# A two-layer decoder trunk on one core: load order, a fourth weight buffer, finer side turns and a later low split

## The chip, the cores and the metric

The kernel runs on one core of a Trainium2 chip. The metric is device time in microseconds for one execution; here the median of three runs. A second figure, the span, is the time from the first to the last instruction of one profiled execution.

## The reference

Input: `x`, 256 tokens of 4096 channels, in float32. Two layers, each with a normalisation ahead of it and a residual sum behind it, then a final normalisation.

```
x = x + even_mixer(rmsnorm(x))     # layer 0
x = x + odd_mixer(rmsnorm(x))      # layer 1
out = rmsnorm(x)

even_mixer(h): u, z_a, qkv, z_b = split(h @ w_in)          # 4096 -> 12288
    y = gelu(s5(u));  y = y * sigmoid(y @ glu_w + b)       # 64 complex state spaces
    o = windowed attention, 8 heads, 3 dilations, merged
    return concat(y * silu(z_a), o * silu(z_b)) @ w_out    # 2048 -> 4096
odd_mixer(h): c_q, c_kv, k_r, k_i, w_i, gate = split(h @ w_in)   # 4096 -> 6336
    indexer: 32 heads score every visible key; each query keeps 64
    32-head attention over the kept latent keys and values
    return (o * silu(gate)) @ w_out                        # 4096 -> 4096
```

`s5(u)` runs a linear complex recurrence over the 256 positions per state: rotate, scan, rotate back, project with C.

## The kernel before

All weight products go through one list of steps. A chunk is up to 1024 output columns of one weight matrix; a step is one chunk's share of 128 rows of the contraction (of 256 or 512 where `kper` is 2 or 4). The chunks in order: `u` (the S5 input), `h0` to `h9` (queries, keys, values and gates of the eight heads, ten 128-column units a head, eight a chunk), `z`, `glu`, `eo0` to `eo3` (even output), `a1`, `a2`, `a3`, `g0`, `iq0` to `iq3` (indexer queries), `g1` to `g3`, then `uq`, `uk`, `uv` for eight groups of four heads, and `oo0` to `oo4` (odd output). Most chunks have 32 steps.

Float32 products are made of three passes. A weight tile `wr` (128 x 1024, 512 KB) is loaded on SyncE's queue (`dma`, L311), rounded to `wh` on ScalarE and the remainder `wl = wr - wh` taken on VectorE (`split`, L322, through `split_to`, L388, at L394 and L399). TensorE then adds `wh` with `xh`, `wl` with `xh`, and `wh` with `xl` into PSUM, for two halves of 128 tokens (`products`, L370): twelve 512-column matmuls a step. `wr`, `wh` and `wl` have three buffers each.

The main loop (L1628) does in step i: split step i+2, load step i+3, let the side jobs advance, and multiply step i. Each engine runs its instructions in this program order.

Everything else is side work, written as generators (`Side`, L222). A job has a rate; `advance` adds the rate to its account and runs the generator to its next `yield` (a turn) for each whole unit. `advance` is left out in the first and the last step of a chunk of eight steps or more, so a 32-step chunk has 30 advances. `finish` runs a job to its end at once. Side matmuls go to two PSUM banks; the chunks rotate over the other six. The side jobs that matter here:

- `x_gen` (L860) brings `x` transposed, in eight pieces of four 128-row tiles, multiplies each piece by the norm weight on POOL, and splits it into `xh`, `xl`. `sums_gen` (L499) loads `x` again as 1 MB tiles `xs` and squares them on ScalarE.
- `s5_main` (L686) handles 32 pairs of groups in batches of four: `s5_tables` and `s5_operands` for the next batch, then per pair two turns on VectorE (rotate; scan and rotate back into `sf`), then the projection with `cpad` and the gelu.
- `even_head` (L764) does rope, scores, softmax, values, transposes into `mhb`/`mlb` for one head, at rate 0.56.
- `idx_all` (L1222) transposes and scores the indexer heads; `mla_all` (L1411) runs the 32 attention heads in five stages, two turns a step.

At a chunk's end its `evac` function empties the PSUM banks; `evac_heads` (L893) first calls `finish` on heads whose place in `ring` is needed. `finish_token` (L1555) is the final norm of 128 tokens.

Of the kernel before, what the change touches and what calls it, by code (L numbers as in the profile page):

```python
# [14 lines left out]
D = 4096  # L15
L = 256
# [108 lines left out]
def lay_out(inp):  # L125
# [71 lines left out]
    a['cpad'] = blockdiag(f['s5_c_re'][0].transpose(0, 2, 1), f['s5_c_im'][0].transpose(0, 2, 1)).reshape(128, 2048)  # L197
# [10 lines left out]
    'mk': (128, 768), 'ident': (128, 128), 'bpad': (8, 128, 256), 'cpad': (128, 2048),  # L208
# [49 lines left out]
def _build(nc, tc, t, debug):  # L258
    from contextlib import ExitStack
    ctx = ExitStack()  # L260
    with ctx:
# [44 lines left out]
        raw, hl = {}, {}  # L306

# [3 lines left out]
        def dma(i, parts=1):  # L311
            c, s, _, _ = steps[i]
            wd = c.kper * c.ncols
            r = st.tile([128, wd], F32, name="wr", tag="wr", bufs=3)
# [7 lines left out]
        def split(i, parts=1):  # L322
# [9 lines left out]
            for k in range(parts):  # L332
                cs = slice(k * wd // parts, (k + 1) * wd // parts)
                split_to(h[:, cs], l[:, cs], r[:, cs])
            hl[i] = (h, l)

# [144 lines left out]
        cpad = big.tile([128, NPAIR, 2, 32], F32, name="cpad", tag="mha")  # L481
# [6 lines left out]
        def x_dma(i, k0=0, k1=4):  # L488
            if k0 == 0:
                xpiece[i] = e.tile([128, 1024], F32, name="xp", tag="SP", bufs=2)  # L490
            DMA.dma_start(xpiece[i][:, k0 * L:k1 * L], t['xT'][i][:, k0 * L:k1 * L])
# [52 lines left out]
        bps = {}  # L544

        def bp_dma(b4):
            bp = e.tile([128, 4, 2, 32], F32, name="bp")
            DMA.dma_start(bp, t['bpad'][b4].rearrange("p (a r c) -> p a r c", a=4, r=2))
            bps[b4] = bp
# [74 lines left out]
        def s5_operands(b4):  # L624
# [6 lines left out]
            for w, (src, second, low) in enumerate(((bk[:, 0:L], 1, 2), (yT[:, b4, :], 2, 1))):  # L631
                A.activation(hi[:, w], src, AF.Copy)
                for j in range(4):
                    A.activation(stk[0:32, w, j, :], src[32 * j:32 * j + 32], AF.Copy)
                for j in range(4):
                    rows = slice(32 * j, 32 * j + 32)
                    V.tensor_tensor(stk[32 * low:32 * low + 32, w, j, :], src[rows], hi[rows, w].bitcast(F32), op=OP.subtract)
                G.tensor_copy(stk[32 * second:32 * second + 32, w], stk[0:32, w])
                yield
# [46 lines left out]
        def s5_main(stage):  # L686
# [10 lines left out]
            V.tensor_scalar(cpad[:, :, 1], cpad[:, :, 1], -1.0, None, op0=OP.mult)  # L697
# [3 lines left out]
            for b4 in range(8):  # L701
# [3 lines left out]
                sfs = []  # L705
                for j in range(4):
# [13 lines left out]
                    V.tensor_tensor(m2[:, 0], bu[:, 1], tab[:, 1], op=OP.mult)  # L720
                    V.tensor_tensor(m2[:, 1], bu[:, 0], tab[:, 1], op=OP.mult)
# [6 lines left out]
                    sf = e.tile([128, 2, L], F32, name="sf", bufs=4)  # L728
                    V.tensor_tensor(sf, sc, cc, op=OP.mult)
                    V.tensor_tensor(m2[:, 0], sc[:, 1], tab[:, 1], op=OP.mult)  # L730
                    V.tensor_tensor(m2[:, 1], sc[:, 0], tab[:, 1], op=OP.mult)
                    V.tensor_tensor(sf[:, 0], sf[:, 0], m2[:, 0], op=OP.subtract)
                    V.tensor_tensor(sf[:, 1], sf[:, 1], m2[:, 1], op=OP.add)
                    sfs.append(sf)
# [6 lines left out]
                for r in range(2):  # L741
                    for j in range(4):
                        rows = slice(32 * j, 32 * j + 32)
                        T.matmul(bk[rows, :L], cpad[:, 4 * b4 + j, r, :], sfs[j][:, r, :], start=(r == 0), stop=(r == 1))
# [5 lines left out]
                A.activation(g1, y, AF.Square)  # L750
                V.tensor_scalar(g1, g1, 0.044715, 1.0, op0=OP.mult, op1=OP.add)
                V.tensor_tensor(g1, g1, y, op=OP.mult)
                A.activation(g2, g1, AF.Tanh, scale=math.sqrt(2.0 / math.pi))

# [9 lines left out]
        def even_head(h, stage):  # L764
# [11 lines left out]
            A.activation(zt, zs, AF.Tanh, scale=0.5)  # L776
            V.scalar_tensor_tensor(zs, zt, 1.0, zs, op0=OP.add, op1=OP.mult)
# [27 lines left out]
            for g in range(3):  # L805
                if g + 1 < 3:
# [9 lines left out]
                         accum_out=sm[:, 1, 1:2])  # L816
            V.reciprocal(sm[:, 2], sm[:, 1])
# [42 lines left out]
        def x_gen():  # L860
            cur['xdone'] = 0
            for i in range(1, 8):
                if i + 1 < 8:
                    x_dma(i + 1)
                p = xpiece[i].rearrange("p (k c) -> p k c", k=4)
                G.tensor_tensor(p, p, spc('ge')[:, 4 * i:4 * i + 4, None].to_broadcast([128, 4, L]), op=OP.mult)
                yield
                for k in (0, 2):
                    kt = slice(4 * i + k, 4 * i + k + 2)
                    split_to(xh[:, kt, :], xl[:, kt, :], p[:, k:k + 2])  # L870
                cur['xdone'] = i
                yield

        def begin_u():
# [3 lines left out]
            cur['x'] = side.add(x_gen(), 1.0)  # L878
# [783 lines left out]
```

## Time and profile before

| | |
|---|---|
| median of 3 runs | 2704.45 us (2704.15 to 2708.99) |
| the profiled execution | 2706.62 us |
| its span | 2704.8 us |
| TensorE busy | 2662.6 us, 98% |
| VectorE, ScalarE, POOL busy | 1709.4, 1224.1, 427.1 us |

The profiled execution's time stands beside its span; the difference is what lies around the span. TensorE's busy time is the union of its matmuls, which are pipelined and overlap, so a busy TensorE may still be slowed within. In the windows view a line gives the stretch, its length, the busy us (and count) of TensorE's matmuls, its weight loads, VectorE, ScalarE and POOL, then granted clock, DMA share and GB/s. Chunk u runs from 5.94 to 107.61 us, h1 to z from 196.85 to 1159.97, iq0 to iq3 from 1652.18 to 1785.14, g2 from 1880.62 to 1967.66, oo4 from 2646.96 to 2692.29. In the waits view, `A <- B: t, n, m` is who waited for whom, the total, the times, the longest.

### The profile page before, as it was taken

What the parts mean: (1) busy time and instruction counts of PE and PEld (TensorE: products, weight loads), DVE (VectorE), ACT (ScalarE), POOL (GpSimd) and SP (SyncE); (2) the same over time, 40 slices, a digit from 0 to 9 for tenths busy, and PEclk for the clock granted to TensorE, in tenths of its full rate; (3) what the DMA queues carried; (4) which work ended last, traced back from release to release, by engine and by line L of the source; (5) the groups of instructions that cost most, each with busy time, mean ns of one, the idle gap of its engine ahead of it and who ended that gap; (6) DMA issues with size and microseconds to landing.
All of it is one profiled execution on the core that took longest, in us unless ns stands there. A gap on an engine that the chain in (4) does not pass through costs nothing.

```text
span 2704.8 us, 33706 instructions
## 1 busy us (share of the span) xinstructions
PE 2662.6 (98%) x12464; PEld 2199.3 (81%) x12464; DVE 1709.4 (63%) x2575; ACT 1224.1 (45%) x1606; POOL 427.1 (16%) x509
## 2 busy tenths in 40 slices
PE   8999999999999999999999999999999999999997
PEld 6787878888887888888888888778888888888886
DVE  5478787877878787465554455556455666654554
ACT  4543444444444444444444444544344555443443
POOL 4214232331323331000000011100000000000000
PEclk9999999999999999999999999999999999999999
DMA  7655545545555455557655556545666444456565
GB/s 267 240 192 182 189 164 179 174 168 170 195 183 171 166 171 178 179 187 264 218 202 189 179 187 223 182 164 191 208 209 206 161 156 163 153 189 226 192 225 197
DMA packets 145061, 516.35 MB, mean 191 GB/s; under 512 B 15872, under 2 KB 17536, under 8 KB 144768
## 3 DMA queue, kind: packets, MB, share of 16 engines
q1 hardware_dynamic: 142368, 504.77, 55.4%
q0 software_dynamic: 2240, 8.39, 0.8%
q8 instruction: 97, 1.59, 0.2%
q10 hardware_dynamic: 288, 1.05, 0.1%
q14 instruction: 68, 0.56, 0.1%
HBM read 501.56 MB, written 12.58 MB: 190 GB/s over the span
## 4 chain that ended last, share of the span: by engine, by line
PE 90%; DVE 4%; DMA 3%; ACT 2%; issue 1%; SPq 0%; POOL 0%; ACTq 0%; DVEq 0%; POOLq 0%
PE bank L382 27%; PE bank L381 27%; PE bank L385 27%; DMA wr<-w_even_in 2%; DVE wl L399 2%; PE bank L367 1%; ACT wh L394 1%; PE bank L1431 1%; DVE sc L727 0%; DMA wr<-w_odd_out 0%; PE bank L834 0%; PE bank L1448 0%; PE bank L787 0%; PE bank L797 0%; DMA wr<-w_iq 0%
## 5 line engine op out<-in xcount | busy, mean ns | idle before, releaser
L399 DVE TENSOR_TENSOR wl<-wr,wh 128x1024 fp32r<-128x1024 f32 (+2 forms) x907 | 1137.4, 1258 | 884.0 <-ACT wh L394 881.1
L394 ACT ACTIVATE wh<-wr 128x1024 fp32r<-128x1024 f32 (+2 forms) x907 | 954.0, 1053 | 1294.6 <-PE bank L385 1041.9
L381 PE MATMUL bank<-wh,xh 128*128 128x512 f32 x1536 | 613.6, 399 | 7.2 <-ACT wh L394 4.1
L382 PE MATMUL bank<-wl,xh 128*128 128x512 f32 x1536 | 602.6, 392 | 13.3 <-DVE wl L399 13.0
L385 PE MATMUL bank<-wh,xl 128*128 128x512 f32 x1536 | 475.0, 390 | 0.0
L382 PEld LDWEIGHTS bank<-wl,xh 128*128 128x128 f32 x1536 | 289.3, 188 | 77.9 <-DVE wl L399 21.5
L381 PEld LDWEIGHTS bank<-wh,xh 128*128 128x128 f32 x1536 | 289.1, 188 | 70.2 <-ACT wh L394 5.9
L385 PEld LDWEIGHTS bank<-wh,xl 128*128 128x128 f32 x1536 | 288.8, 188 | 62.6
L381 PE MATMUL bank<-wh,x2h 128*128 128x512 f32 (+1 forms) x832 | 318.7, 383 | 0.0
L382 PE MATMUL bank<-wl,x2h 128*128 128x512 f32 (+1 forms) x832 | 316.5, 380 | 0.0
L385 PE MATMUL bank<-wh,x2l 128*128 128x512 f32 (+1 forms) x832 | 254.0, 380 | 0.0
L381 PE MATMUL bank<-wh,oh 128*128 128x512 f32 x488 | 191.9, 393 | 0.0
L382 PE MATMUL bank<-wl,oh 128*128 128x512 f32 x488 | 190.4, 390 | 1.1 <-DVE wl L399 1.1
L385 PEld LDWEIGHTS bank<-wh,x2l 128*128 128x128 f32 x832 | 156.5, 188 | 30.2
L381 PEld LDWEIGHTS bank<-wh,x2h 128*128 128x128 f32 x832 | 156.5, 188 | 29.6
L382 PEld LDWEIGHTS bank<-wl,x2h 128*128 128x128 f32 x832 | 156.6, 188 | 29.4
L385 PE MATMUL bank<-wh,ol 128*128 128x512 f32 x488 | 158.9, 389 | 0.0
L382 PEld LDWEIGHTS bank<-wl,oh 128*128 128x128 f32 x488 | 91.7, 188 | 20.9 <-DVE wl L399 2.3
L385 PEld LDWEIGHTS bank<-wh,ol 128*128 128x128 f32 x488 | 91.6, 188 | 19.3
L381 PEld LDWEIGHTS bank<-wh,oh 128*128 128x128 f32 x488 | 91.7, 188 | 18.9 <-ACT v L450 0.4
L381 PE MATMUL bank<-wh,cb_h 128*128 128x512 f32 (+1 forms) x224 | 87.9, 393 | 0.0
L382 PE MATMUL bank<-wl,cb_h 128*128 128x512 f32 (+1 forms) x224 | 84.0, 375 | 0.0
(395 smaller groups left out, 3069.2 us busy)
## 6 DMA issues: line engine op xcount, KB each, us to landing
wr<-w_even_in SPq DMA_DIRECT2D x383, 512.0 KB, 3.4
wr<-w_odd_in SPq DMA_DIRECT2D x192, 512.0 KB, 3.2
wr<-w_odd_out SPq DMA_DIRECT2D x128, 512.0 KB, 3.5
wr<-w_even_out SPq DMA_DIRECT2D x64, 512.0 KB, 3.8
wr<-w_iq SPq DMA_DIRECT2D x48, 512.0 KB, 3.4
wr<-w_uq SPq DMA_DIRECT2D x48, 512.0 KB, 3.4
wr<-w_uv SPq DMA_DIRECT2D x16, 512.0 KB, 3.3
wr<-w_uk SPq DMA_DIRECT2D x16, 384.0 KB, 3.1
```

Of the source, the lines that this page charges most:

```text
L367: T.matmul(c.banks[0][b], hp, hls[k][:, b * 512:b * 512 + 512], start=f0 and k == 0, stop=l0 and k == 1)
L381: T.matmul(acc, xh[:, tok], h[:, b0 + o:b0 + o + n_], start=f0, stop=False)
L382: T.matmul(acc, xh[:, tok], l[:, b0 + o:b0 + o + n_], start=False, stop=False)
L385: T.matmul(acc, xl[:, tok], h[:, b0 + o:b0 + o + n_], start=False, stop=l0)
L394: A.activation(hi, src, AF.Copy)
L399: V.tensor_tensor(lo, src, hi.bitcast(F32), op=OP.subtract)
L1431: T.matmul(bk[:, 128:384], o[:, 0, 128:256], o[:, 1, :], start=True, stop=True)
```

## The change

- Start: the first piece of `x` and the norm weights are loaded on ScalarE's queue; the second weight tile is loaded and split in halves, right behind the first; the rest of `sp` comes later. `wr` has four buffers, and step i loads step i+4.
- `split` issues only `wh`; the subtract for `wl` (`low`) is issued behind the side jobs' turn of the same step.
- `x_gen` leaves out POOL's multiply; the norm weight is applied in the split of each quarter, two quarters a turn, at rate 0.7 and first in the list of jobs.
- S5: turns are cut smaller and the rate is 0.96 in place of 0.5; C comes in eight loads `cb` beside those of B, negated on POOL; `sf` becomes one tile `sfs`; the operand's low part is subtracted once for 128 rows and copied in 32-row pieces on ScalarE.
- `even_head` has two more `yield`s at the same rate. The indexer's rate is 1.0, and a group of four waits until four steps after its `evac`.
- `oo4` loads its residual at k = 8; five of six small steps of the final norm move from POOL to VectorE.

```diff
@@ -304,6 +306,7 @@
         raw, hl = {}, {}
+        now = [0]
@@ -311,7 +314,7 @@
             wd = c.kper * c.ncols
-            r = st.tile([128, wd], F32, name="wr", tag="wr", bufs=3)
+            r = st.tile([128, wd], F32, name="wr", tag="wr", bufs=4)
@@ -331,8 +334,16 @@
                 cs = slice(k * wd // parts, (k + 1) * wd // parts)
-                split_to(h[:, cs], l[:, cs], r[:, cs])
+                A.activation(h[:, cs], r[:, cs], AF.Copy)
             hl[i] = (h, l)
+
+            def low():
+                for k in range(parts):
+                    cs = slice(k * wd // parts, (k + 1) * wd // parts)
+                    V.tensor_tensor(l[:, cs], r[:, cs], h[:, cs].bitcast(F32), op=OP.subtract)
+            if parts > 1:
+                low()
+            return low
@@ -478,7 +489,7 @@
         mk = cp.tile([128, 3, 256], F32, name="mk", tag="mk")
-        cpad = big.tile([128, NPAIR, 2, 32], F32, name="cpad", tag="mha")
+        sfs = big.tile([128, 4, 2, L], F32, name="sfs", tag="mha")
@@ -488,7 +499,7 @@
                 xpiece[i] = e.tile([128, 1024], F32, name="xp", tag="SP", bufs=2)
-            DMA.dma_start(xpiece[i][:, k0 * L:k1 * L], t['xT'][i][:, k0 * L:k1 * L])
+            (A if i == 0 else DMA).dma_start(xpiece[i][:, k0 * L:k1 * L], t['xT'][i][:, k0 * L:k1 * L])
@@ -541,12 +552,14 @@
-        bps = {}
+        bps, cbs = {}, {}
...
             DMA.dma_start(bp, t['bpad'][b4].rearrange("p (a r c) -> p a r c", a=4, r=2))
-            bps[b4] = bp
+            cb = e.tile([128, 4, 2, 32], F32, name="cb", bufs=3)
+            DMA.dma_start(cb, t['cpad'][b4].rearrange("p (a r c) -> p a r c", a=4, r=2))
+            bps[b4], cbs[b4] = bp, cb
@@ -629,14 +642,14 @@
             for w, (src, second, low) in enumerate(((bk[:, 0:L], 1, 2), (yT[:, b4, :], 2, 1))):
-                A.activation(hi[:, w], src, AF.Copy)
-                for j in range(4):
-                    A.activation(stk[0:32, w, j, :], src[32 * j:32 * j + 32], AF.Copy)
-                for j in range(4):
-                    rows = slice(32 * j, 32 * j + 32)
-                    V.tensor_tensor(stk[32 * low:32 * low + 32, w, j, :], src[rows], hi[rows, w].bitcast(F32), op=OP.subtract)
+                lo = e.tile([128, L], F32R, name="ulo")
+                split_to(hi[:, w], lo, src)
+                yield
+                for k, part in ((0, hi[:, w]), (low, lo)):
+                    for j in range(4):
+                        A.activation(stk[32 * k:32 * k + 32, w, j, :], part[32 * j:32 * j + 32].bitcast(F32), AF.Copy)
+                    yield
                 G.tensor_copy(stk[32 * second:32 * second + 32, w], stk[0:32, w])
-                yield
@@ -694,7 +707,6 @@
             yield from s5_tables(0)
-            V.tensor_scalar(cpad[:, :, 1], cpad[:, :, 1], -1.0, None, op0=OP.mult)
@@ -702,7 +714,7 @@
                         yield
-                sfs = []
+                G.tensor_scalar(cbs[b4][:, :, 1], cbs[b4][:, :, 1], -1.0, None, op0=OP.mult)
@@ -718,6 +730,7 @@
                     V.tensor_tensor(m2[:, 0], bu[:, 1], tab[:, 1], op=OP.mult)
+                    yield
@@ -725,13 +738,14 @@
                         V.tensor_tensor_scan(sc[:, r], mg, m1[:, r], 0.0, op0=OP.mult, op1=OP.add)
-                    sf = e.tile([128, 2, L], F32, name="sf", bufs=4)
+                    yield
+                    sf = sfs[:, j]
...
                     V.tensor_tensor(m2[:, 0], sc[:, 1], tab[:, 1], op=OP.mult)
+                    yield
...
                     V.tensor_tensor(sf[:, 1], sf[:, 1], m2[:, 1], op=OP.add)
-                    sfs.append(sf)
@@ -741,16 +755,18 @@
                         rows = slice(32 * j, 32 * j + 32)
-                        T.matmul(bk[rows, :L], cpad[:, 4 * b4 + j, r, :], sfs[j][:, r, :], start=(r == 0), stop=(r == 1))
+                        T.matmul(bk[rows, :L], cbs[b4][:, j, r, :], sfs[:, j, r, :], start=(r == 0), stop=(r == 1))
...
                 A.activation(g1, y, AF.Square)
+                yield
...
                 A.activation(g2, g1, AF.Tanh, scale=math.sqrt(2.0 / math.pi))
+                yield
@@ -774,6 +790,7 @@
             A.activation(zt, zs, AF.Tanh, scale=0.5)
+            yield
@@ -814,6 +831,7 @@
                          accum_out=sm[:, 1, 1:2])
+            yield
@@ -862,29 +880,26 @@
                     x_dma(i + 1)
-                p = xpiece[i].rearrange("p (k c) -> p k c", k=4)
-                G.tensor_tensor(p, p, spc('ge')[:, 4 * i:4 * i + 4, None].to_broadcast([128, 4, L]), op=OP.mult)
-                yield
                 for k in (0, 2):
-                    kt = slice(4 * i + k, 4 * i + k + 2)
-                    split_to(xh[:, kt, :], xl[:, kt, :], p[:, k:k + 2])
-                cur['xdone'] = i
-                yield
+                    split_all([(xh[:, 4 * i + j, :], xl[:, 4 * i + j, :], xpiece[i][:, j * L:(j + 1) * L], spc('ge', 4 * i + j))
+                               for j in (k, k + 1)])
+                    if k == 2:
+                        cur['xdone'] = i
+                    yield
...
             cur['sums'] = side.add(sums_gen(), 0.8)
-            cur['x'] = side.add(x_gen(), 1.0)
+            cur['x'] = side.add(x_gen(), 0.7, first=True)
...
             evac_scaled(c, lambda q: stage[:, q], rstd)
-            DMA.dma_start(cpad, t['cpad'].rearrange("p (a r c) -> p a r c", a=NPAIR, r=2))
             DMA.dma_start(mk, t['mk'].rearrange("p (g c) -> p g c", g=3))
-            s5['job'] = side.add(s5_main(stage), 0.5)
+            s5['job'] = side.add(s5_main(stage), 0.96)
@@ -1256,7 +1271,7 @@
-                        for _ in range(5):
+                        while now[0] < od['iat'] + 4:
@@ -1274,7 +1289,7 @@
                     od['iready'] = od['itr'] = 0
-                    od['ij'] = side.add(idx_all(), 1.4)
+                    od['ij'] = side.add(idx_all(), 1.0)
@@ -1283,7 +1298,7 @@
                 stage = o.tile([128, 1536], F32, name="iqs", tag="Q", bufs=2)
-                lo = o.tile([64, 2, 512], F32, name="iqlo")
+                lo = o.tile([64, 2, 512], F32, name="iqlo", tag="sq")
@@ -1296,7 +1311,7 @@
                 od['iq', i] = stage
-                od['iready'] = i + 1
+                od['iready'], od['iat'] = i + 1, now[0]
@@ -1509,7 +1524,7 @@
                     side.step(u['j'])
-                if k == 20:
+                if k == (8 if i == 4 else 20):
@@ -1560,12 +1575,12 @@
             V.tensor_reduce(v, ss[:, q, :], op=OP.add, axis=mybir.AxisListType.X)
-            G.tensor_scalar(v, v, 1.0 / D, EPS, op0=OP.mult, op1=OP.add)
+            V.tensor_scalar(v, v, 1.0 / D, EPS, op0=OP.mult, op1=OP.add)
             G.tensor_tensor(y, v, mhalf[:, 0:1], op=OP.pow)
-            G.tensor_tensor(a, y, y, op=OP.mult)
-            G.tensor_tensor(a, a, v, op=OP.mult)
-            G.tensor_scalar(a, a, -0.5, 1.5, op0=OP.mult, op1=OP.add)
-            G.tensor_tensor(y, y, a, op=OP.mult)
+            V.tensor_tensor(a, y, y, op=OP.mult)
+            V.tensor_tensor(a, a, v, op=OP.mult)
+            V.tensor_scalar(a, a, -0.5, 1.5, op0=OP.mult, op1=OP.add)
+            V.tensor_tensor(y, y, a, op=OP.mult)
@@ -1604,14 +1619,15 @@
         a0, b0 = SP['ge']
-        DMA.dma_start(sp[:, a0:b0], t['sp'][:, a0:b0])
         x_dma(0, 0, 1)
+        A.dma_start(sp[:, a0:b0], t['sp'][:, a0:b0])
         dma(0, 2)
+        dma(1, 2)
         x_dma(0, 1, 4)
-        DMA.dma_start(sp[:, b0:], t['sp'][:, b0:])
-        dma(1)
...
         x_dma(1)
+        dma(3)
+        DMA.dma_start(sp[:, b0:], t['sp'][:, b0:])
@@ -1623,18 +1639,21 @@
         x_split(0, 1, 4)
-        split(1)
+        split(1, 2)
...
             c, s, first, last = steps[i]
-            if i + 2 < n:
-                split(i + 2)
-            if i + 3 < n:
-                dma(i + 3)
+            now[0] = i
+            low = split(i + 2) if i + 2 < n else None
+            if i + 4 < n:
+                dma(i + 4)
...
                 side.advance()
+
+            if low:
+                low()
```

## Rows read from the trace of the kernel before

**Rows 1.** The page: busy time, share of the span and count of each engine.

```profile
PE 2662.6 (98%) x12464; PEld 2199.3 (81%) x12464; DVE 1709.4 (63%) x2575; ACT 1224.1 (45%) x1606; POOL 427.1 (16%) x509
```

**Rows 2.** Windows by stage: u; h1 to z; iq0 to iq3; g2; oo4.

```profile
5.94:107.61 101.67, 92.83 (x387) 72.83 (x385) 56.35 (x59) 52.37 (x69) 45.55 (x75) 0.98 0.73 262
...
196.85:1159.97 963.12, 951.41 (x4471) 779.46 (x4470) 735.56 (x1243) 420.95 (x527) 266.81 (x275) 1.00 0.53 176
...
1652.18:1785.14 132.96, 129.57 (x584) 103.38 (x582) 80.84 (x96) 71.64 (x98) 18.72 (x14) 1.00 0.60 197
1880.62:1967.66 87.04, 87.04 (x386) 72.10 (x384) 42.96 (x39) 37.30 (x39) 1.13 (x2) 1.00 0.60 206
...
2646.96:2692.29 45.33, 43.84 (x192) 35.77 (x191) 22.53 (x23) 17.95 (x20) 4.08 (x8) 1.00 0.54 178
```

**Rows 3.** Waits of TensorE in u: total us, times, longest.

```profile
PE bank L382 <- DVE wl L399: 4.5, 6, 1.5
PE bank L381 <- ACT wh L394: 4.1, 3, 2.7
```

**Rows 4.** Waits in u of ScalarE and of SyncE's queue.

```profile
ACT wh L394 <- DMA wr<-w_even_in: 37.2, 21, 6.4
...
SPq L319 <- DVE wl L399: 42.6, 24, 6.6
```

**Rows 5.** Waits of TensorE in h1 to z.

```profile
PE bank L382 <- DVE wl L399: 8.5, 7, 1.8
PE bank L381 <- DVE ring L456: 3.1, 4, 1.0
```

**Rows 6.** Timeline of VectorE, an S5 turn: start, us, line, operation, tiles.

```profile
245.74 1.27 DVE L727 TENSOR_TENSOR_SCAN sc<-s5mag,m 128x256 f32<-128x256 f32 x2
...
247.98 0.42 DVE L731 TENSOR_TENSOR m<-sc,tab 128x256 f32<-128x256 f32 x1
...
248.65 1.28 DVE L733 TENSOR_TENSOR sf<-sf,m 128x256 f32<-128x256 f32 x1
249.86 3.19 DVE L399 TENSOR_TENSOR wl<-wr,wh 128x1024 fp32r<-128x1024 f32 x2
```

**Rows 7.** Timeline of TensorE at the start.

```profile
1.44 5.45 PE L1622 MATMUL bank<-warm 128*128 128x512 f32 x6 [1.44 <-DVE warm L1620]
5.94 1.19 PE L381 MATMUL bank<-wh,xh 128*128 128x512 f32 x1
...
10.70 0.49 PE L381 MATMUL bank<-wh,xh 128*128 128x512 f32 x1 [1.05 <-ACT wh L394]
11.95 0.50 PE L382 MATMUL bank<-wl,xh 128*128 128x512 f32 x1 [0.76 <-DVE wl L399]
```

**Rows 8.** Instructions on tile xp: count, ns minimum, median, maximum.

```profile
L399 DVE TENSOR_TENSOR xl<-xp,xh x14: 678/688/2384, 18.0 to 59.7; 128x512 fp32r<-128x512 f32 x14
...
L401 DVE SCALAR_TENSOR_TENSOR xl<-xp,sp,xh x4: 481/482/485, 4.5 to 8.8; 128x256 fp32r<-128x256 f32 x4
```

**Rows 9.** Groups of VectorE by form: busy us, mean ns, idle before, releaser.

```profile
L399 DVE TENSOR_TENSOR wl<-wr,wh 128x1024 fp32r<-128x1024 f32 x881 | 1113.0, 1268 | 853.0 <-ACT wh L394 850.1
...
L637 DVE TENSOR_TENSOR stk<-yT,uhl 32x256 fp32r<-32x256 f32 x32 | 21.9, 683 | 0.5
...
L1440 DVE RECIPROCAL usm<-usm 128x2 f32<-128x2 f32 x32 | 5.3, 166 | 33.7 <-ACT uS L1439 33.7
...
L839 DVE SCALAR_TENSOR_TENSOR ob<-bank,sm,ring 128x128 f32<-128x128 f32 x16 | 4.8, 342 | 0.0
```

**Rows 10.** Groups of ScalarE by form, the same columns.

```profile
L394 ACT ACTIVATE wh<-wr 128x1024 fp32r<-128x1024 f32 x881 | 932.6, 1059 | 1262.4 <-PE bank L385 1012.3 <-DMA wr<-w_even_in 109.1 <-issue 36.2
...
L634 ACT ACTIVATE stk<-yT 32x256 fp32r<-32x256 f32 x32 | 13.2, 412 | 0.3
...
L1438 ACT ACTIVATE uS<-uS,usm 128x128 f32<-128x128 f32 x32 | 12.9, 402 | 75.7 <-DVE usm L1437 75.7
```

**Rows 11.** Timeline of VectorE in the last norm.

```profile
2696.38 1.42 DVE L1574 TENSOR_SCALAR x<-x,rstd 128x1024 f32<-128x1024 f32 x2 [2.04 <-POOL rstd L1568]
```

More of the change, by code (lines that the diff above doesn't have):

```diff
@@ L196, in lay_out @@
         blockdiag(f['s5_b_re'][0], f['s5_b_im'][0]).reshape(128, 8, 256).transpose(1, 0, 2))
-    a['cpad'] = blockdiag(f['s5_c_re'][0].transpose(0, 2, 1), f['s5_c_im'][0].transpose(0, 2, 1)).reshape(128, 2048)
+    a['cpad'] = np.ascontiguousarray(
+        blockdiag(f['s5_c_re'][0].transpose(0, 2, 1), f['s5_c_im'][0].transpose(0, 2, 1))
+        .reshape(128, 8, 256).transpose(1, 0, 2))
     a['glub'] = f['s5_glu_b'][0].reshape(1, 1024)
@@ L207 @@
     'w_uk': (KVR * 3072,), 'w_uv': (KVR * D,), 'w_odd_out': (D * D,), 'sp': (128, SPW),
-    'mk': (128, 768), 'ident': (128, 128), 'bpad': (8, 128, 256), 'cpad': (128, 2048),
+    'mk': (128, 768), 'ident': (128, 128), 'bpad': (8, 128, 256), 'cpad': (8, 128, 256),
     'glub': (1, 1024), 'gkidx': (1, HD), 'gfin': (1, D),
```

## The prediction

> **What bounds the kernel now.** I read the busy times first. TensorE is busy 2662.6 us of the span of 2704.8 [rows 1], so only a stretch where TensorE stands still can give time back. Next, the table by stage. Chunk g2 is the measure of a clean chunk: 384 full matmuls, no side work, 87.04 us, TensorE busy throughout, 0.2267 us a matmul [rows 2]. Chunk u has the same 384 and takes 101.67 us: 14.6 lost. Chunks h1 to z lose 963.12 - 951.41 = 11.7 us, iq0 to iq3 132.96 - 129.57 = 3.4, and oo4, with 192 matmuls, 45.33 - 43.5 = 1.8 [rows 2].
>
> Then who TensorE waits for. In u it is `wl` from VectorE (4.5 us) and `wh` from ScalarE (4.1); the rest of the 14.6 is half hidden, because the busy times of pipelined matmuls overlap [rows 3]. ScalarE in turn waits 37.2 us there for `wr` to land, and SyncE's queue waits 42.6 us for VectorE to free a `wr` buffer before it can ask for the next tile [rows 4]. So u is short of buffers, not of bandwidth: it moves 262 GB/s x 101.67 us = 26.6 MB at a DMA share of 0.73; at share 1 that is 359 GB/s and 74 us, under the 87.04 us of matmuls [rows 2].
>
> In h1 to z the waits are 8.5 us for `wl` and 3.1 for the evacuation into `ring`, eleven waits of up to 1.8 us [rows 5]. VectorE's timeline shows how one arises: a whole S5 turn from 245.74 (two scans) to the last `sf` at 248.65, and only at 249.86 the next low splits, two back to back in 3.19 us [rows 6]. That turn takes 4.1 us, against a step of 12 x 0.2267 = 2.72.
>
> **Start: two queues, order of loads.** Nothing moves the first product: three warm matmuls (six passes) hold TensorE from 1.44 us for 5.45 us, and the first `xh` product is recorded at 5.94, inside their end [rows 7]. What counts is that the second weight tile now goes ahead of the rest of `x`, of `sp` and of `ident`: before, its first product stood at 10.70 after a wait of 1.05 us, and the `wl` product behind it at 11.95 after another 0.76 [rows 7]. That is 1.8 us; I take 2, with the bubbles on either side. The load issues moved to ScalarE's queue stand ahead of ScalarE's first work, which waits for data anyway: nothing.
>
> The Trainium skill (DMA: Bandwidth & Descriptors, "Issuing engines are not separate DMA queues") speaks against the two queues: loads from any engine end on the same 16 DMA engines and interleave, and a second issuer saves only the time of the issue. The trace before has its first loads on one queue and can't show it. By that rule the two queues alone are worth nothing in the sum, as the warm matmuls cover the issue time; and the 2 us are those of the order.
>
> **Chunk u: fourth `wr` buffer, slower `x`, no POOL multiply.** A `wr` tile is freed when its low split is done, and the next must land and be split before its matmul. A fourth buffer gives each load one more step, 2.72 us, ahead of waits that were 37.2 us over 21 occurrences, 1.8 us each [rows 4]. Seven POOL multiplies ahead of the `x` splits disappear; one of the fourteen `xl` splits took 2.38 us against a median of 0.69 [rows 8]. The scale moves into splits by quarter, 0.48 us on VectorE [rows 8] and about as much on ScalarE; two a turn at rate 0.7 make 0.7 us a step on each. With 1.06 and 1.27 us for a weight split [rows 9, 10], both engines stay under 2.72 us a step. Bounds: below, half of what waits now, 6 us with the start's 2; above, all 14.6 but some 0.8 that the warm-up costs inside u, so 13.8. I take 10.5, nearer the upper end, since it is buffers that are waited for.
>
> **Low split behind the side turn; turns cut small.** VectorE takes its side turn while ScalarE makes `wh`, instead of idling. S5 turns shrink from 4.1 us to at most 0.42 + 0.42 + 1.28 = 2.1 us, or two scans in 1.27 [rows 6]. With a low split of 1.27 [rows 9] that is 3.4 us, against the two steps (5.4 us) between the release of a `wh` buffer and its next use; so the 8.5 us of `wl` waits should nearly go, and the `ring` waits come of the same backlog. The overall schedule stays: S5 has 154 turns at rate 0.5, which is 308 advances; then 298 at 0.96, which is 310, of 330 in eleven chunks. VectorE also sheds the 32-row subtracts into `stk` (21.9 us for the half that reads `yT`) for sixteen full ones [rows 9], and ScalarE gains 64 copies of 0.41 us, 26 us, covered: it is busy 421 of 963 us there [rows 2, 10]. Gain 8; bounds 4 and 11.7.
>
> **What it costs: two more turns per head.** `even_head` keeps its rate 0.56 but gets two more yields: 18 turns instead of 16. A chunk has 30 advances (its first and last step have none), so 16.8 turns. Heads 0, 1, 4, 5 and 7 have exactly one chunk before an evacuation calls `finish` on them: 16 turns fit, 18 don't. Their last two turns (probabilities times values, then the transposes of `ob`) now run back to back between two chunks, where TensorE must wait for two `ob` multiplies of 0.34 us [rows 9] and the hand-overs, with the evacuation queued behind them on VectorE. Before, a step lay between, and this was free. Price of each: nothing, if a later step makes it up; 0.8, two multiplies and an estimated 0.1 for hand-overs; 1.6, if the evacuation comes late too, as its longest wait of 1.0 [rows 5] suggests. I take 0.8, so 4 us; bounds 0 and 8.
>
> **C by batches.** One 1 MB load becomes eight small ones, and one negation on VectorE eight on POOL, which is 28% busy there (266.81 of 963.12) [rows 2]; `sfs` has the four slots of the old `sf`. Nothing.
>
> **Indexer.** Rate 1.0 instead of 1.4 never puts a transpose turn and a score turn into one step, where the score needs the bank that ScalarE is still emptying. Against it, side work is spread over more steps, so the stream is broken more often. Bounds 0 and 3.4 [rows 2]; I take 2.
>
> **Last chunk and norm.** Loading the last residual at k = 8 takes it off the last weight loads: 1.5 of oo4's 1.8 us [rows 2], bounds 0.5 and 1.8. In the norm, VectorE waits 2.04 us for six POOL steps [rows 11]; five of them move to VectorE, where a small operation takes 0.17 [rows 9], while the power stays on POOL. I take 0.5, bounds 0.2 and 0.7. Multi-head attention and output keep their work: 0, bounds -2 and 1.5.
>
> **Sum.** 10.5 + 8 - 4 + 2 + 1.5 + 0.5 = 18.5 us. The profiled execution took 2706.62 us with a span of 2704.8; the median of the three runs is 2704.45. 2704.45 - 18.5 = 2686.
>
> **Rivals.**
> *u stays as starved as it is.* The loads of `x` and `xs` hold the queue, and a fourth tile only waits longer in it. For it: 21 waits on landing [rows 4]. Against: a share of 0.73. Then only 2 of the 10.5 remain: gain 10, 2694.5.
> *The bursts eat the head gain.* All five cost 1.6, and the `ring` waits stay: 8 - 3 - 8 = -3 in place of +4. Gain 11.5, 2693.
> *Slower: the low split is caught behind a side turn that waits.* In multi-head attention's softmax turn VectorE waits 33.7 us over 32 heads for ScalarE's exponential, 1.05 each [rows 9], and ScalarE waits 75.7 us, 2.4 each, for VectorE ahead of it [rows 10]. The low split, so far first, now stands behind this turn. The chain is two exponentials of 0.40, that 1.05 us wait, a low of 1.27 [rows 9, 10] and, by my estimate, 1.7 us of maxima, second turn and hand-overs: 4.8 us. The point that decides is two steps, 5.4 us, plus their side matmuls, up to 2 more. If each of 32 heads comes 1.2 us past it, that is 38 us: 2704.45 - 18.5 + 38 = 2724. Against it: ScalarE's 2.4 us shrink once the low is out of VectorE's way.
> *More than forecast.* The bursts are free and all waits go: 13.8 + 11.7 + 2 + 1.5 + 0.5 = 29.5, 2675.
>
> **Chances.** Forecast 0.55 (its own range 2680 to 2692), u starved 0.18, bursts 0.14, more 0.07, slower 0.06. A change under 0.2% (5.4 us) can't be told from none. Of the slower case 0.05 lies beyond that and 0.01 within; of u starved and bursts, 0.04 is both at once (2701.5) and within. So faster 0.90, same 0.05, slower 0.05. The range 2675 to 2698 leaves out the slower case, both rivals at once, and the far end of "more".
>
> **What would show it.** u near 91 us, with ScalarE's waits for `wr` a fraction of 37.2; the first product still near 5.94, and no wait near 10.70. In h1 to z few `wl` waits above 0.5 us, but five chunk ends with some 0.8 us ahead of the `ob` transposes. In the indexer no wait at the score's second half. The prediction is wrong if u stays above 97 us, if the bursts cost over 1.6 each, or if waits for `wl` appear in multi-head attention.

## The result, and the profile after

The changed kernel takes 2680.13 us (median of 4 runs, 2679.9 to 2681.61) against 2705.93 for the kernel before beside it: ratio 0.9908, 95% interval 0.9897 to 0.992. The forecast was 2686, range 2675 to 2698. The span fell from 2704.8 to 2678.5 us.

The page of the changed kernel, the row that answers to [rows 1]:

```profile
PE 2655.3 (99%) x12464; PEld 2199.5 (82%) x12464; DVE 1665.9 (62%) x2551; ACT 1258.8 (47%) x1685; POOL 411.2 (15%) x500
```

The same 12464 matmuls; what fell is mostly the time around and within them. Windows of the changed kernel, columns as in [rows 2]: u; h0; h1 to z; iq0 to iq3; g2 (g1 lies between these two); oo4. A chunk runs from its first main matmul to the next chunk's first. All these stretches have a granted clock of 1.00.

```profile
6.86:94.68 87.82, 87.67 (x385) 72.19 (x385) 55.53 (x74) 56.49 (x84) 31.96 (x68) 1.00 0.87 312
94.68:187.15 92.47, 90.68 (x406) 73.69 (x404) 63.79 (x129) 44.29 (x57) 26.91 (x27) 1.00 0.55 186
187.15:1138.81 951.66, 948.94 (x4469) 780.21 (x4468) 689.90 (x1161) 444.15 (x580) 255.92 (x270) 1.00 0.54 180
...
1631.63:1762.96 131.33, 128.45 (x584) 103.61 (x582) 80.71 (x96) 71.23 (x98) 18.66 (x14) 1.00 0.61 197
1857.10:1944.14 87.04, 87.04 (x386) 72.07 (x384) 42.95 (x39) 37.30 (x39) 1.13 (x2) 1.00 0.63 206
2623.03:2666.32 43.29, 43.29 (x192) 35.85 (x191) 23.20 (x28) 17.74 (x20) 3.13 (x3) 1.00 0.53 180
```

u needs 87.82 us, next to g2's 87.04, at 312 GB/s in place of 262. It ends at 94.68 and not 107.61: 12.9 us. h0 to z take 1138.81 - 94.68 = 1044.1 against 1159.97 - 107.61 = 1052.4: 8.2 us (S5 now does more in h0 and less later, so only the sum can be compared). iq0 to the end of g1 take 1857.10 - 1631.63 = 225.5 against 1880.62 - 1652.18 = 228.4: 3.0. oo4 has 43.29 against 45.33: 2.0. The last window goes from 12.5 to 12.2 us.

Waits of TensorE in h0 to z, then in the whole kernel the longest of all (changed kernel; total us, times, longest):

```profile
PE bank L862 <- DVE ob L857: 2.2, 5, 0.4
PE bank L393 <- DVE wl L343: 1.0, 3, 0.5
PE bank L642 <- POOL bb L632: 1.0, 1, 1.0
```

```profile
PE bank L1246 <- POOL iqs L474: 2.9, 3, 1.0
```

Against [rows 5]: the 8.5 us for `wl` are 1.0, those for `ring` are gone. The five waits for `ob`, none before, are the five heads whose last two turns run in `finish`. In the indexer three new waits stand for the rope on POOL. In u, ScalarE and SyncE's queue, against [rows 4]:

```profile
ACT wh L337 <- DMA wr<-w_even_in: 2.2, 2, 1.2
...
SPq L322 <- DVE wl L343: 59.2, 31, 3.6
```

ScalarE's wait for landing is 2.2 us in place of 37.2. SyncE's queue still waits for free buffers, longer than before (59.2 us against 42.6), and next to nothing waits for it in turn: a wait of a queue is only a cost where its data are missed.

### The profile page after: what moved, and what is told of

It reads as the page before. It is cut to its first block, busy times and chain, and to the rows that moved or that the text cites. A ratio compares the mean times of both kernels' runs of the same rounds, so it can differ in the third digit from the quotient of the medians.

```text
span 2678.5 us, 33786 instructions
## 1 busy us (share of the span) xinstructions
PE 2655.3 (99%) x12464; PEld 2199.5 (82%) x12464; DVE 1665.9 (62%) x2551; ACT 1258.8 (47%) x1685; POOL 411.2 (15%) x500
## 4 chain that ended last, share of the span: by engine, by line
PE 93%; DVE 3%; ACT 1%; issue 1%; POOL 1%; DMA 0%; ACTq 0%; POOLq 0%; DVEq 0%
PE bank L393 29%; PE bank L392 28%; PE bank L396 28%; DVE wl L343 1%; PE bank L378 1%; ACT wh L337 1%; PE bank L1446 1%; PE bank L852 0%; PE bank L804 0%; PE bank L1463 0%; PE bank L814 0%; PE bank L758 0%; PE bank L843 0%; PE bank L726 0%; ACT x2r L1566 0%
## 5 line engine op out<-in xcount | busy, mean ns | idle before, releaser
L392 PEld LDWEIGHTS bank<-wh,oh 128*128 128x128 f32 x488 | 91.7, 188 | 18.5
```

The lines of the kernel that those rows point to most:

```text
L392: T.matmul(acc, xh[:, tok], h[:, b0 + o:b0 + o + n_], start=f0, stop=False)
```

## The experiments

All runs are changes to the changed kernel, but for `before_x`. In the table "u ends" is h0's first matmul, and the stretches are those of the windows above, from each run's profile.

| run | median us | ratio to before (95%) | u ends | h0 to z | iq0 to g1 |
|---|---|---|---|---|---|
| before | 2705.93 | 1 | 107.61 | 1052.4 | 228.4 |
| changed | 2680.13 | 0.9908 (0.9897 to 0.992) | 94.68 | 1044.1 | 225.5 |
| three_bufs | 2698.12 | 0.9971 (0.996 to 0.9981) | 97.55 | 1053.0 | 227.8 |
| x_as_before | 2690.49 | 0.995 (0.9935 to 0.9965) | 105.73 | 1043.9 | 225.4 |
| x_rate | 2680.12 | 0.9899 (0.9884 to 0.9914) | 94.55 | 1043.8 | 225.4 |
| before_x | 2698.01 | 0.9973 (0.9961 to 0.9984) | 99.84 | 1052.9 | 228.2 |
| one_queue | 2682.61 | 0.9921 (0.9906 to 0.9936) | 96.68 | 1044.9 | 225.4 |
| low_first | 2692.96 | 0.996 (0.9946 to 0.9974) | 94.69 | 1056.3 | 225.4 |
| turns_coarse | 2707.16 | 1.0004 (0.9995 to 1.0014) | 94.59 | 1070.6 | 225.4 |
| low_first_coarse | 2717.61 | 1.0043 (1.0028 to 1.0058) | 94.84 | 1081.3 | 225.4 |
| lumps_same_pace | 2693.11 | 0.9953 (0.9939 to 0.9967) | 94.93 | 1058.9 | 225.5 |
| head_rate | 2677.12 | 0.9887 (0.987 to 0.9905) | 94.50 | 1040.9 | 225.4 |
| idx_five | 2676.91 | 0.9887 (0.9872 to 0.9902) | 94.59 | 1044.2 | 222.0 |
| all_three | 2672.74 | 0.9878 (0.9864 to 0.9893) | 94.52 | 1040.5 | 221.9 |

The medians of the kernel before beside the runs are 2705.2 to 2705.9 us. A profile shows one execution: three_bufs' lies 3.4 us below its median and lumps_same_pace's 2.2 above, the others within 1.6. So three_bufs' profiled span, 2692.9, is 14.4 above the changed kernel's, and its median 18.0 above.

**Chunk u: buffers, or x?** `three_bufs`:

```diff
-            r = st.tile([128, wd], F32, name="wr", tag="wr", bufs=4)
+            r = st.tile([128, wd], F32, name="wr", tag="wr", bufs=3)
...
-        dma(3)
...
-            if i + 4 < n:
-                dma(i + 4)
+            if i + 3 < n:
+                dma(i + 3)
```

> The changed kernel with three wr buffers again (step i loads step i+3); start order, slower x, low split behind the turn all kept. Theory 'buffers' (the fourth buffer is what freed chunk u): u goes from 87.8 us back to 94 or more, and ScalarE's waits for wr in u rise from near nothing to 20 us or more; the whole kernel 2687 to 2692 against 2680. Rival 'order and slower x' (the loads merely came in a better order and x no longer crowded them): u stays under 90 us, the whole kernel under 2683.

u ends only 2.9 us later, at 97.55: the theory 'buffers' falls for u. Neither forecast is met in full: u takes 90.92 us, under the theory's 94 and over the rival's 90, and 2698.12 is outside both ranges. ScalarE's waits there do come back, 27.3 us, but split over 21 occasions they are mostly made up. The fourth buffer earns the greater part of its 14.4 us elsewhere: h0 to z 8.9 us, the indexer 2.3. ScalarE's waits for `wr` from 94 to 1139 us, first with three buffers, then in the changed kernel:

```profile
ACT wh L337 <- DMA wr<-w_even_in: 73.5, 34, 7.6
```

```profile
ACT wh L337 <- DMA wr<-w_even_in: 23.0, 8, 5.2
```

There a `wr` buffer comes free late, because its low split now stands behind a turn, and the fourth buffer covers that. `x_as_before`:

```diff
+                p = xpiece[i].rearrange("p (k c) -> p k c", k=4)
+                G.tensor_tensor(p, p, spc('ge')[:, 4 * i:4 * i + 4, None].to_broadcast([128, 4, L]), op=OP.mult)
+                yield
                 for k in (0, 2):
-                    split_all([(xh[:, 4 * i + j, :], xl[:, 4 * i + j, :], xpiece[i][:, j * L:(j + 1) * L], spc('ge', 4 * i + j))
-                               for j in (k, k + 1)])
-                    if k == 2:
-                        cur['xdone'] = i
-                    yield
+                    kt = slice(4 * i + k, 4 * i + k + 2)
+                    split_to(xh[:, kt, :], xl[:, kt, :], p[:, k:k + 2])
+                cur['xdone'] = i
+                yield
...
-            cur['x'] = side.add(x_gen(), 0.7, first=True)
+            cur['x'] = side.add(x_gen(), 1.0)
```

> The changed kernel with x brought as before (POOL's multiply, rate 1.0, last in the list of jobs), four wr buffers kept. Theory 'buffers': u 88 to 90 us, the whole 2680 to 2683. Rival 'order and slower x': u 94 us or more, the whole 2687 or more.

With four buffers, u ends at 105.73, 11 us later: the rival holds. POOL's, ScalarE's and VectorE's timelines of this run, and TensorE's waits in u:

```profile
48.10 0.29 POOL L546 TENSOR_SCALAR w<-w 128x32 f32<-128x32 f32 x1
48.35 3.74 POOL L884 TENSOR_TENSOR xp<-xp,sp 128x1024 f32<-128x1024 f32 x2
```

```profile
50.28 1.15 ACT L405 ACTIVATE xh<-xp 128x512 fp32r<-128x512 f32 x2 [5.82 <-DMA wr<-w_even_in]
51.33 1.04 ACT L337 ACTIVATE wh<-wr 128x1024 fp32r<-128x1024 f32 x1
```

```profile
50.94 2.31 DVE L410 TENSOR_TENSOR xl<-xp,xh 128x512 fp32r<-128x512 f32 x2 [7.89 <-ACT xh L405]
53.18 2.35 DVE L343 TENSOR_TENSOR wl<-wr,wh 128x1024 fp32r<-128x1024 f32 x2
```

```profile
PE bank L393 <- DVE wl L343: 7.4, 6, 5.4
```

POOL works off S5's exponential (some twenty 128x32 operations, the last at 48.10), and only then the multiply of `x`, two of them in 3.74 us, so the first ends near 48.35 + 1.87 = 50.2. ScalarE's `xh` begins at 50.28 after 5.82 us of waiting. The view puts that wait down to a `wr` load, which `xh` does not read; it ends when POOL is done. `wh` stands behind `xh` on ScalarE, `wl` behind `xl` on VectorE, and TensorE waits 5.4 us at once.

The same is in the kernel before. The view behind [rows 4] has a second row, for `xh`, put down to `wr` as well; POOL's and ScalarE's timelines show that `xh` begins when the first of two multiplies ends, near 51.51 + 1.87 = 53.4:

```profile
ACT xh L394 <- DMA wr<-w_even_in: 4.7, 1, 4.7
```

```profile
51.51 3.74 POOL L866 TENSOR_TENSOR xp<-xp,sp 128x1024 f32<-128x1024 f32 x2
53.43 1.15 ACT L394 ACTIVATE xh<-xp 128x512 fp32r<-128x512 f32 x2 [4.67 <-DMA wr<-w_even_in]
```

The wait has a second price that neither the prediction nor a run was made for: TensorE's granted clock fell with it. Windows of x_as_before, then of the kernel before:

```profile
52.80:59.60 6.80, 5.16 (x12) 4.10 (x13) 5.16 (x6) 3.65 (x8) 0.00 (x0) 0.50 0.50 162
```

```profile
57.90:61.30 3.40, 3.40 (x9) 2.67 (x8) 2.89 (x4) 2.64 (x5) 0.00 (x0) 0.50 0.67 210
```

A granted clock of 0.50 is the lower level, 1.2 GHz. In x_as_before it fell while TensorE stood, 5.42 us up to 54.44; the eleven matmuls from there to 59.30 take 4.86 us, where at g2's 0.2267 they would take 2.5. In the kernel before, the fall follows TensorE's two longest waits of [rows 3]. In chunk u of the changed kernel and of `before_x` the clock is 1.00.

The multiply also holds VectorE. POOL, VectorE and TensorE in x_as_before:

```profile
34.66 2.06 POOL L884 TENSOR_TENSOR xp<-xp,sp 128x1024 f32<-128x1024 f32 x1 [2.86 <-DMA xp<-xT]
34.88 2.92 DVE L343 TENSOR_TENSOR wl<-wr,wh 128x1024 fp32r<-128x1024 f32 x1
37.85 0.50 PE L393 MATMUL bank<-wl,xh 128*128 128x512 f32 x1 [0.78 <-DVE wl L343]
```

This `wl`, begun while the multiply runs, takes 2.92 us against a mean of 1.27 in [rows 9], and ends 1.08 us after the multiply does. Each of the four `wl` of this run that began so took 2.7 to 2.9 us. In the kernel before, the three long `xl` splits (2.38, 2.38 and 1.70 us, [rows 8] has the longest) began so too and ended 0.55 us after the multiply. So the 11 us of this run are, in the main, a wait of 5.4, 2.4 of slower clock behind it, and some 3 us lost before it, where the shorter waits for `wl` stand (2.0 of the 7.4).

To part this from the rate, `x_rate`:

```diff
-            cur['x'] = side.add(x_gen(), 0.7, first=True)
+            cur['x'] = side.add(x_gen(), 1.0)
```

> The changed kernel with x_gen at rate 1.0 and last in the list, but still scaled in the split, without POOL. Theory 'POOL's queue' (what cost 11 us with x brought as before was POOL's multiply standing behind S5's preparation on POOL, with ScalarE's xh waiting for it and wh behind that): u within 2 us of 87.8, the whole 2680 to 2682. Rival 'rate' (x loaded too early crowds the weights): u 92 us or more, the whole 2685 or more.

No difference (94.55): the rate does nothing, POOL's multiply did it. What neither run parts from the multiply is that x_as_before splits a whole piece in one turn, the changed kernel half a piece. `before_x` makes the same point from the other side, with this in the kernel before:

```diff
-                p = xpiece[i].rearrange("p (k c) -> p k c", k=4)
-                G.tensor_tensor(p, p, ..., op=OP.mult)
-                yield
                 for k in (0, 2):
-                    kt = slice(4 * i + k, 4 * i + k + 2)
-                    split_to(xh[:, kt, :], xl[:, kt, :], p[:, k:k + 2])
-                cur['xdone'] = i
-                yield
+                    split_all([(xh[:, 4 * i + j, :], xl[:, 4 * i + j, :], xpiece[i][:, j * L:(j + 1) * L], spc('ge', 4 * i + j))
+                               for j in (k, k + 1)])
+                    if k == 2:
+                        cur['xdone'] = i
+                    yield
```

> The kernel before with one change: x scaled in its split, rate 1.0, no POOL multiply; three buffers, old start, old order. Theory 'POOL's queue': u from 101.67 to 94 to 97 us (the rest stays with the start and the buffers), the whole faster by 5 to 8 us than before. Rival (without the fourth buffer the loads hold u up all the same): u 99.5 us or more, the whole within 2.5 us of before.

u takes 94.46 us and ends at 99.84 instead of 107.61, 7.8 us of the 12.9, with three buffers and the old start. The theory holds.

**The two queues.** `one_queue`:

```diff
-            (A if i == 0 else DMA).dma_start(xpiece[i][:, k0 * L:k1 * L], ...)
+            DMA.dma_start(xpiece[i][:, k0 * L:k1 * L], ...)
...
-        A.dma_start(sp[:, a0:b0], t['sp'][:, a0:b0])
+        DMA.dma_start(sp[:, a0:b0], t['sp'][:, a0:b0])
```

> The changed kernel with its first loads all on SyncE's queue, in the same program order. Theory (the second queue brings nothing, the warm matmuls hide the issue time): first product within 0.3 us of its 6.86 us, the whole within 1 us of 2680. Rival (two queues start the loads sooner): first product, or the second tile's first one, later by 1 us or more, the whole 2681.5 or more.

u ends 2.0 us later, and the rival holds by its second condition, the second tile's product. The two ratios' intervals overlap, so this rests on one profile of `one_queue`; on the other side eight profiles with the changed start end u between 94.50 and 94.93. The first product comes sooner, at 5.53, but TensorE stands 1.58 us ahead of 11.57. TensorE, ScalarE and the load issues of `one_queue`, then of the changed kernel:

```profile
1.17 0.42 SPq L1623 DMA_DIRECT2D sp<-sp  x1
...
3.41 0.51 ACT L407 ACTIVATE xh<-xp,sp 128x256 fp32r<-128x256 f32 x1 [1.19 <-DMA sp<-sp]
...
9.70 1.30 ACT L407 ACTIVATE xh<-xp,sp 128x256 fp32r<-128x256 f32 x3 [2.79 <-DMA xp<-xT]
...
11.57 0.50 PE L392 MATMUL bank<-wh,xh 128*128 128x512 f32 x1 [1.58 <-ACT wh L337]
```

```profile
1.17 0.45 ACTq L1623 DMA_DIRECT2D sp<-sp  x1
...
5.78 0.51 ACT L407 ACTIVATE xh<-xp,sp 128x256 fp32r<-128x256 f32 x1 [2.15 <-DMA sp<-sp]
...
6.86 0.58 PE L392 MATMUL bank<-wh,xh 128*128 128x512 f32 x1
7.27 1.31 ACT L407 ACTIVATE xh<-xp,sp 128x256 fp32r<-128x256 f32 x3
```

On one queue the rest of `x` lands behind both weight tiles, and ScalarE, in order, holds the second tile's `wh` behind it. On two queues it is issued earlier and needs no wait at 7.27, while the tiny norm weights, second on ScalarE's queue, land late, and the first `xh` starts at 5.78; with one queue it starts at 3.41. The norm weights are issued at 1.17 in both, so here it is not the time of the issue that differs.

**Order and length of the turns.** `low_first` and `turns_coarse`:

```diff
-            if parts > 1:
-                low()
-            return low
+            low()
+            return None
```

```diff
                     V.tensor_tensor(m2[:, 0], bu[:, 1], tab[:, 1], op=OP.mult)
-                    yield
...
-                    yield
                     sf = sfs[:, j]
...
                     V.tensor_tensor(m2[:, 0], sc[:, 1], tab[:, 1], op=OP.mult)
-                    yield
...
-            s5['job'] = side.add(s5_main(stage), 0.96)
+            s5['job'] = side.add(s5_main(stage), 0.652)
```

> The changed kernel with the low split issued right behind its wh again, ahead of the side turn; fine turns kept. Theory 'fine turns do it' (what delayed wl was the length of a turn): h0 to z up by 2 us at most, the whole 2680 to 2682. Rival 'the order does it': VectorE again idles for wh before each low split, h0 to z up by 5 us or more, the whole 2685 or more, waits of TensorE for wl near the 8.5 us of before.

> The changed kernel with S5's pair cut into two turns again (rate 0.652, so that it ends at the same step); low split behind the turn, four buffers kept. Theory 'the order does it' (the low split behind the turn, with a fourth buffer, is enough): h0 to z within 2 us of 1044.1, the whole 2680 to 2682.5. Rival 'short turns are needed': h0 to z up by 5 us or more, the whole 2685 or more, with waits for wl in the scan turns.

Both rivals hold. With the low split first, h0 to z take 12.2 us more. It is not `wl` that is waited for, though, as expected, but other work: VectorE's `ring`, POOL's `bb`, ScalarE's `wh`. VectorE's low splits in h0 to z (busy, mean ns, idle before), `low_first` and then the changed kernel:

```profile
L343 DVE TENSOR_TENSOR wl<-wr,wh 128x1024 fp32r<-128x1024 f32 x352 | 451.5, 1285 | 277.6 <-ACT wh L337 276.5
```

```profile
L343 DVE TENSOR_TENSOR wl<-wr,wh 128x1024 fp32r<-128x1024 f32 x352 | 448.9, 1278 | 178.7 <-ACT wh L337 178.0
```

The order saves VectorE 98 us of idling behind `wh`; TensorE's stretch gains 12.2 us. Coarse turns cost 26.5 us. `low_first_coarse`, both diffs together:

> The changed kernel with both undone: low split right behind its wh, and S5's pair in two turns at rate 0.652; four buffers kept. It completes the two by two. Theory 'only together' (coarse turns hurt only a low split that stands behind them, fine turns help nothing when the low split goes first): h0 to z between 1050 and 1058, near low_first's 1056, the whole 2685 to 2694. Rival 'coarse turns cost by themselves': h0 to z 1065 or more, near turns_coarse's 1071, the whole 2700 or more.

h0 to z 1081.3: the rival holds and 'only together' falls. That is 28.9 us more than in the kernel before, which has the low split first and coarse turns too, and no run parts what makes it; the pace, below, is one difference. But these coarse runs changed two things. With two turns a pair at rate 0.652 a pair takes 3.1 steps, with five at 0.96 it takes 5.2 (and four in the kernel before). `lumps_same_pace` keeps five turns and puts the work into two of them:

```diff
                     V.tensor_tensor(m2[:, 0], bu[:, 1], tab[:, 1], op=OP.mult)
-                    yield
...
                     yield
+                    yield
...
-                    yield
                     sf = sfs[:, j]
...
                     V.tensor_tensor(m2[:, 0], sc[:, 1], tab[:, 1], op=OP.mult)
-                    yield
...
                     V.tensor_tensor(sf[:, 1], sf[:, 1], m2[:, 1], op=OP.add)
                     yield
+                    yield
+                    yield
```

> The changed kernel with the work of S5's pair in two lumps again (rotate; scan and rotate back), but with the same five turns a pair at rate 0.96, three of them empty, so that a pair takes the same 5.2 steps. turns_coarse had also changed the pace: 3.1 steps a pair. Theory 'pace' (what hurt there was pairs following each other too fast for VectorE, not the length of a lump): h0 to z 1044 to 1048, the whole 2680 to 2684. Rival 'length of a turn' (a low split behind a lump of 4 us comes too late): h0 to z 1054 or more, the whole 2690 or more.

h0 to z 1058.9, the rival: of turns_coarse's 26.5 us, 14.7 go with the length of a turn and the other 11.8 with the pace, taken in this order. In medians the two shares are 13.0 and 14.1. TensorE's waits for `wl` in the two runs, lumps first:

```profile
PE bank L393 <- DVE wl L343: 11.4, 14, 2.7
```

```profile
PE bank L393 <- DVE wl L343: 21.0, 28, 2.6
```

VectorE's timeline of lumps_same_pace from 932 us shows how: the work from the scans to the last add runs without a break for 4.1 us, then three low splits in a row.

```profile
932.06 1.26 DVE L740 TENSOR_TENSOR_SCAN sc<-s5mag,m 128x256 f32<-128x256 f32 x2
...
934.98 1.28 DVE L746 TENSOR_TENSOR sfs<-sfs,m 128x256 f32<-128x256 f32 x1
936.18 4.88 DVE L343 TENSOR_TENSOR wl<-wr,wh 128x1024 fp32r<-128x1024 f32 x3
```

**The two new waits.** `head_rate` and `idx_five`:

```diff
-                        cur['head', h] = side.add(even_head(h, half), 0.56, first=True)
+                        cur['head', h] = side.add(even_head(h, half), 0.61, first=True)
```

```diff
-                        while now[0] < od['iat'] + 4:
+                        while now[0] < od['iat'] + 5:
```

> The changed kernel with even_head at rate 0.61, so that 18 turns fit into 30 advances. Theory (the five bursts cost what TensorE waits there for ob, 2.2 us, and a little for weight loads): those five waits vanish, h0 to z shorter by 2 to 3.5 us, the whole 2676.5 to 2678. Rival (the waits only move, since the same work falls on fewer steps): h0 to z within 1 us.

> The changed kernel with the indexer's group waiting five steps in place of four behind its evac. Theory (the three waits of 1.1 us for the rope on POOL come of starting one step too early): they vanish, iq0 to g1 shorter by 2 to 3.3 us, the whole 2677 to 2678.5. Rival (the last score of each group then falls into the next chunk and is waited for there): no gain, within 1 us.

Both hold: 3.2 us in h0 to z, where the five waits for `ob` are gone, and 3.5 us in the indexer, where no wait of TensorE is left. `all_three` adds them, and loads the first norm weights first on SyncE's queue:

```diff
-        x_dma(0, 0, 1)
-        A.dma_start(sp[:, a0:b0], t['sp'][:, a0:b0])
+        DMA.dma_start(sp[:, a0:b0], t['sp'][:, a0:b0])
+        x_dma(0, 0, 1)
```

> The changed kernel with even_head at 0.61, the indexer's group waiting five steps, and the first norm weights loaded first on SyncE's queue in place of second on ScalarE's. Theory: the gains add, 3.1 + 3.4 us, and 0.5 to 1 us at the start since the norm weights no longer land behind the first weight tile; the whole 2672.5 to 2674. Rival for the start (the weight tile then lands later by as much): no gain there, the whole 2674 to 2675.

2672.74 us, the fastest: the first two add up. The third brings the first product forward to 6.39, but u ends at 94.52, within the 94.50 to 94.93 of the other runs with this start: in the profile it gains nothing. The median is 1.2 us below what the other two add up to, inside the theory's range and not the rival's, so its worth is not settled.

## Why the prediction was right, and where it was off

- *Sum*: 18.5 us forecast; 25.8 between the medians, 26.3 in the span. Every term had its sign; u and h0 to z were too small. That the time still fell near the forecast is in part luck, as the next point shows.
- *u, 2 + 8.5 us*: 12.9 measured, near the bound of 13.8. The size was nearly right and the cause was not. The step "it is buffers that are waited for" failed: the fourth buffer is worth 2.9 us in u. POOL's multiply, which the prediction named beside one slow `xl` split and gave no price of its own, is worth 11 us undone and 7.8 alone; the change removed it, so the sum came out. The mistake was to take ScalarE's 37.2 us of [rows 4] for a cost. 29.3 of them are still there in `before_x` and 27.3 in `three_bufs`, where u is 7.2 and 10.8 us shorter: waits that are mostly made up before TensorE needs the tile. The greatest single loss came behind the 4.7 us of `xh`: two steps, from 49.39 to 61.82, took 12.43 us for 5.44, half of the 14.6 lost in u, with the granted clock at 0.50 in the last 3.4 of them, which the prediction's sum has no term for. The 0.8 us that it allows for a warm-up inside u has no row behind it; the changed kernel's first step takes 3.50 us (6.86 to 10.36) for 2.72, and no run shows why.
- *Start*: that nothing moves the first product failed: it moved from 5.94 to 6.86, since the first `xh` now waits for the norm weights until 5.78. The wait near 10.70 is gone, as forecast, and no run measures the order of loads alone. That the two queues are worth nothing failed in one profile: 2.0 us. The Trainium skill (DMA: Bandwidth & Descriptors, "Issuing engines are not separate DMA queues") has loads from several engines interleave on the same DMA engines, which agrees: the norm weights, issued at 1.17 on either queue, are waited for until 5.78 beside the weights' queue and until 3.41 ahead of the weights in one queue. That a second issuer saves only issue time does not agree here; it also changes what lands first. The rest of `x` gains by issue time as well.
- *h0 to z, 8 - 4 us*: 8.2 net. Nearly all of 11.7 came back (gross 8.2 + 3.2 = 11.4), and the five bursts cost 3.2 us, 0.65 each, for 0.8 forecast. That short turns behind `wh` are needed both ways is shown by `low_first` and `lumps_same_pace`. The fourth buffer, priced at nothing here, carries 8.9 us of it, by three_bufs' profile.
- *Indexer, 2*: 3.0, and the old wait at the score is gone, but a new one of 2.9 us for the rope took part of the gain back, which the prediction did not see.
- *Last chunk 1.5, norm 0.5*: 2.0 and 0.4.
- *Rivals*: u did not stay starved and the bursts did not eat the gain. The slower one, a low split behind a turn that waits, did not show in multi-head attention: the stretch from g2 to the first product of oo0 takes 445.35 us in both kernels, without a wait of TensorE for `wl`. Its mechanism is real, as the coarse runs show for S5.
- *Open*: the cost of coarse pace by itself was seen only through the difference of two runs, and the fourth buffer was taken away only with all else in place; what it would bring to the kernel before was not run.

## What to carry to other kernels

When a wait is put down to a load, look whether the waiting instruction reads it; if not, look for the engine whose work ends at that moment, here POOL, with unrelated small work ahead of the multiply in its queue. And price a wait by what TensorE loses, not by its total. In this kernel a split that is off the path by two steps gained by standing behind the side work of its step, but only where that work came in short turns at an even pace, and with one more buffer for what is now freed later. When a job gets more turns, its rate must follow: count turns against the advances it has before it is finished by force.

## What was not expected of the hardware

Which queue a load is issued on changed when it was there by microseconds: behind two weight tiles on one queue the rest of `x` let ScalarE start at 9.70, on a second queue at 7.27; a 16 KB load, issued at 1.17 in both, let ScalarE's first `xh` start only at 5.78 when it was second on that queue, against 3.41 with one queue.

A subtract of VectorE that began while POOL's 128x1024 multiply ran did not end before it: `wl` ended 1.08 us after the multiply (1.10 in one case) and `xl` 0.55, in every such case in before and x_as_before.
